# The root of the norms in four VectorE operations instead of six, and the last block's rows multiplied by the final weights before their root is known

## The chip, the cores and the metric

The kernel runs on one core of one Trainium2 chip. The metric is the device time of one execution in microseconds (us), and kernels are compared by the medians of several. A core has a matrix engine (TensorE, here PE, whose weight loads are shown as PEld), three engines for element-wise work (VectorE or DVE, ScalarE or ACT, GpSimd or POOL), and an engine that issues most of the transfers (SyncE or SP). Each engine runs its own list of instructions in a fixed order and waits at an instruction until its inputs and its output buffer are free.

## The reference

One layer of a decoder with 1,024 tokens of width 1,024 and 16 learned meta tokens ahead of them:

```python
def rmsnorm(x, g):
    x32 = x.astype(jnp.float32)
    y = x32 * lax.rsqrt(jnp.mean(x32 * x32, axis=-1, keepdims=True) + EPS)
    return (y * g.astype(jnp.float32)).astype(x.dtype)
...
        h = h + hybrid_mixer(rmsnorm(h, attn_norm_g[l]), pos, topk, w_in[l], mla_q_norm_g[l], w_uq[l],
                             mla_kv_norm_g[l], w_ukv[l], w_o[l])
        h = h + swiglu(rmsnorm(h, ffn_norm_g[l]), w_gate[l], w_up[l], w_down[l])
    h = rmsnorm(h, final_norm_g)
    return h[:, N_META:t]
```

`hybrid_mixer` has two groups of heads on one input projection: eight heads of latent attention (MLA, dense and causal, with a norm of its own on each latent), and eight heads of sparse attention (DSA), in which an indexer scores all keys and each query keeps the 256 best. The outputs of both go through one output projection `w_o`. `swiglu` is the feed-forward part (FFN) with a hidden width of 2,816. What matters for this change is `rmsnorm`: per row, the mean of the squares plus EPS, its inverse root, and the product with the weights `g`.

## The kernel before

The 1,024 rows are eight blocks of 128, one row for each partition. Blocks 0 to 2 are called A here (`BLK_A`), blocks 3 to 7 B (`BLK_B`). The stages follow each other like this in the profile: the norm of the input, the projections and the index scores, with the first searches for the 256 best keys (0 to about 330 us); attention of A, and its output projection (to about 500); attention of B with the FFN of A interleaved (to about 966, the last product of the FFN of A is added at 977.94); the output projection of B (to about 1070); the FFN of B by seven products of block sums (to about 1490); the last norms (to the end). All products are made of three fp32r matmuls (`three`, L195 to L198), for which each operand is split into a rounded part and a rest (`split`, L186 to L193): ACT writes the rounded part (`wH`, `woh`, `us` and so on), and POOL or DVE subtracts it (`wL`, `wol`).

**The root.** `rstd` (L151 to L162) takes the sum of squares `ss` and gives 1/sqrt(ss/n + EPS). DVE makes the mean (L155), ACT its square root (L156), DVE the reciprocal r (L157), and then one step of Newton's iteration in four operations, r(1.5 - 0.5 v r r) (L158 to L161). These tiles have one column a block (128x1), so the operations are short. It is called 40 times: in `norm_in` (L278) for the nine norms of the input (tile `rs`), in `latent` (L517) for 17 latents (tile `rsc`), in `out_proj` (L1060) once for the three blocks of A together (width 3) and once for each block of B, and in `last_norm` (L1285) for the eight blocks. Its users: `norm_in` and `latent` scale rows; `out_proj` writes `un` (L1065, 128x512, twice a block), which PE transposes (L1068) as the input of the FFN; `last_norm` scales the rows that go out (L1290 to L1294).

**The last norm.** For each half of a block ACT sums squares (`yj`, L1279). When both halves are there, DVE adds the sums (L1284) and `rstd` follows. The first 512 columns are scaled and weighted by DVE in one operation (L1293), the second 512 by ACT (L1290) and POOL (L1291), except in the last block, where DVE does both halves. For A this happens at about 970 to 1000 us, for B at the end.

**The search.** The 256 best keys of a query are found bit by bit: a pass counts the keys above a bound, and the bound moves. For blocks 6 and 7 ACT makes the passes (L382, tile `js`, with two small operations L383 and L385 between), and DVE ends the search (L445 to L458), after which the bias of that block's DSA scores is known: PE makes scores (L790), DVE adds the bias and takes the extreme (L792), ACT makes the exponentials (L799), DVE and POOL split them into fp16 parts (`hl`, L819 and L821), a transfer transposes them (`pT`), and PE multiplies by the values (L830 to L832).

**The output projection of B.** `w_o` comes in 32 pieces of 128x256 through two buffers `wor`, each through one chain: transfer, ACT (`woh`, L188), POOL (`wol`, L191), matmuls.

**What sets the order.** The code names no order across stages beyond its loops and generators. The program is built with the framework's own timeline scheduling, which estimates when each operation could run and writes every engine's list by that. So a change of the number or form of operations anywhere can put other instructions into another order on every engine, even on those that the change doesn't name.

## Time and profile before

| | us |
|---|---|
| median of 3 runs | 1516.27 |
| lowest and highest of them | 1514.63, 1522.13 |
| profiled execution, its time | 1515.98 |
| profiled execution, span from first to last instruction | 1514.2 |
| mean granted clock of TensorE, share of full speed | 0.972 |

The rows of the profile are times of one execution, counted from its first instruction. "Busy" is the sum of durations on an engine; matmuls overlap, so that the busy time of a matmul in a row is longer than its distance to the next one. The view of waits shows how long an engine stood at an instruction and which other instruction ended that. The chain of work that ended last is followed back from the end of the program.

### The profile page before, as it was taken

What the parts mean: (1) busy time and instruction counts of PE and PEld (TensorE: products, weight loads), DVE (VectorE), ACT (ScalarE), POOL (GpSimd) and SP (SyncE); (2) the same over time, 40 slices, a digit from 0 to 9 for tenths busy, and PEclk for the clock granted to TensorE, in tenths of its full rate; (3) what the DMA queues carried; (4) which work ended last, traced back from release to release, by engine and by line L of the source; (5) the groups of instructions that cost most, each with busy time, mean ns of one, the idle gap of its engine ahead of it and who ended that gap; (6) DMA issues with size and microseconds to landing.
All of it is one profiled execution on the core that took longest, in us unless ns stands there. A gap on an engine that the chain in (4) does not pass through costs nothing. (4 is left out here: it accounts for less than half of the span.)

```text
span 1514.2 us, 29979 instructions
## 1 busy us (share of the span) xinstructions
PE 1405.1 (93%) x10320; PEld 1295.3 (86%) x10320; DVE 1105.3 (73%) x2714; ACT 922.9 (61%) x2264; POOL 892.8 (59%) x1185
## 2 busy tenths in 40 slices
PE   6999998899989899899999999888799999999996
PEld 5999998897778789798888888788789999999995
DVE  6878989948886875957766666736676777777766
ACT  5666578897889889788544444434544444444444
POOL 2564555212404588687878778643846666666653
PEclk9999999999999799999999999998899999999999
DMA  6113265224434688687879998741222222222211
GB/s 177 55 48 85 73 143 134 52 89 131 130 102 123 146 193 166 147 171 175 182 157 222 200 203 181 188 140 50 65 62 84 84 84 84 79 76 83 84 56 70
DMA packets 353737, 180.74 MB, mean 119 GB/s; under 512 B 196560, under 2 KB 341344, under 8 KB 353584
## 3 DMA queue, kind: packets, MB, share of 16 engines
q1 hardware_dynamic: 353584, 178.82, 47.7%
q8 instruction: 81, 1.33, 0.4%
q14 instruction: 72, 0.59, 0.1%
HBM read 120.77 MB, written 21.30 MB: 94 GB/s over the span
## 5 line engine op out<-in xcount | busy, mean ns | idle before, releaser
L191 POOL TENSOR_TENSOR wL<-raw,wH 128x256 fp32r<-128x256 f32 x352 | 286.1, 846 | 59.0 <-ACT wH L188 55.3
L821 POOL TENSOR_TENSOR hl<-pd,hl 128x260 f16<-128x260 f32 (+5 forms) x256 | 168.8, 689 | 71.1 <-ACT hl L817 31.8
L191 POOL TENSOR_TENSOR wsl<-raw,wsh 128x256 fp32r<-128x256 f32 x132 | 120.3, 940 | 94.1 <-ACT wsh L188 53.6
L196 PE MATMUL b<-wh,uH 128*128 128x256 f32 (+3 forms) x568 | 169.2, 298 | 6.3 <-DVE mlo L318 3.2
L198 PE MATMUL b<-wh,uL 128*128 128x256 f32 (+3 forms) x568 | 168.5, 297 | 0.0
L197 PE MATMUL b<-wl,uH 128*128 128x256 f32 (+3 forms) x568 | 168.1, 296 | 0.1
L188 ACT ACTIVATE wH<-raw 128x1024 fp32r<-128x1024 f32 x88 | 91.8, 1054 | 79.4 <-PE b L198 20.0
L196 PE MATMUL b<-us,wsh 128*128 128x320 f32 x440 | 136.1, 313 | 1.5 <-DVE oh L1251 1.1
L197 PE MATMUL b<-us,wsh 128*128 128x320 f32 x440 | 136.4, 311 | 0.0
L198 PE MATMUL b<-us,wsl 128*128 128x320 f32 x440 | 134.2, 310 | 0.0
L196 PE MATMUL b<-ua,wH 128*128 128x384 f32 x352 | 122.1, 347 | 3.4 <-ACT wH L188 3.4
L382 ACT ACTIVATE js<-sc,bs 128x528 bf16<-128x528 int16 (+7 forms) x128 | 120.9, 945 | 4.7 <-DVE sc L437 2.4
L197 PE MATMUL b<-ua,wH 128*128 128x384 f32 x352 | 121.2, 344 | 0.0
L198 PE MATMUL b<-ua,wL 128*128 128x384 f32 x352 | 120.7, 344 | 0.1
L196 PE MATMUL b<-wH,hH 128*128 128x512 f32 x282 | 113.5, 403 | 3.9 <-DVE oh L1171 2.1
L196 PEld LDWEIGHTS b<-wh,uH 128*128 128x128 f32 x568 | 108.7, 191 | 8.3 <-DVE mlo L318 3.9
L197 PE MATMUL b<-wL,hH 128*128 128x512 f32 x282 | 112.1, 397 | 0.0
L198 PE MATMUL b<-wH,hL 128*128 128x512 f32 x282 | 110.1, 398 | 0.4 <-DVE hL L193 0.4
L197 PEld LDWEIGHTS b<-wl,uH 128*128 128x128 f32 x568 | 108.8, 191 | 0.5 <-DVE wl L193 0.3
L198 PEld LDWEIGHTS b<-wh,uL 128*128 128x128 f32 x568 | 108.6, 191 | 0.4 <-DVE uL L193 0.2
L1240 DVE TENSOR_TENSOR oh<-b,oh 128x512 f32<-128x512 f32 x110 | 74.5, 685 | 46.3 <-PE b L198 45.4
L799 ACT ACTIVATE pd<-pd,sm 128x528 f32<-128x528 f32 (+4 forms) x80 | 75.7, 946 | 48.6 <-DVE sm L797 46.1
(410 smaller groups left out, 4848.0 us busy)
## 6 DMA issues: line engine op xcount, KB each, us to landing
raw<-in_w_gate SPq DMA_DIRECT2D x44, 512.0 KB, 4.0
raw<-in_w_up SPq DMA_DIRECT2D x44, 512.0 KB, 4.1
raw<-in_w_down SPq DMA_DIRECT2D x44, 512.0 KB, 3.7
wor<-in_w_o SPq DMA_DIRECT2D x64, 128.0 KB, 2.5
wraw<-in_w_in SPq DMA_DIRECT2D x40, 128.0 KB, 2.4
vh<-v_x SPq DMA_DIRECT2D x16, 288.0 KB, 3.8
xt<-in_x SPq DMA_DIRECT2D x8, 512.0 KB, 4.4
ks_x<-st SPq DMA_DIRECT2D x32, 128.0 KB, 2.1
```

The source lines that it names most:

```text
L188: S.activation(h, src, AF.Copy)
L191: G.tensor_sub(l[:, c], src[:, c], h[:, c])
L196: PE.matmul(o, lh, rh, start=first, stop=False, **kw)
L197: PE.matmul(o, lh, rl, start=False, stop=False, **kw)
L198: PE.matmul(o, ll, rh, start=False, stop=last, **kw)
L382: S.activation(act_junk()[:, :n_keys(b)], y[b], AF.Sign, bias=cols[0], accum_out=cnt)
L799: S.activation(pb, pb, AF.Exp, bias=mn, scale=-1.0, accum_out=z)
L821: G.tensor_sub(pl_[:, c], pb[:, c], ph[:, c])
L1240: V.tensor_add(oh[t][:, cs], po, oh[t][:, cs])
```

## The change

In `rstd` the mean is made with the factor -4 (and -4 EPS), ACT's square root takes it with scale -1, and the reciprocal is then half of 1/sqrt. The Newton step becomes two fused operations (`scalar_tensor_tensor`, two steps of arithmetic on one pass): r r v in one, and (that + 3) r in the other. With width 3 the first of them stays two products. So DVE runs four operations instead of six in 39 of the 40 calls, and five in the one of width 3: 79 fewer.

In `last_norm`, for the last block (7) alone, the rows are multiplied by `gl` into a buffer `raw` of the FFN's weights before the root is made: DVE columns 0 to 511 and 768 to 1023, POOL columns 512 to 767. When the root is there, DVE scales columns 0 to 511 and ACT columns 512 to 1023. The list of DVE has 78 instructions fewer in all (2,528 after 2,606), ACT and POOL have one more each.

```diff
-        V.tensor_scalar(v[:, 0], ss, 1.0 / n, EPS, op0=OP.mult, op1=OP.add)
-        S.activation(v[:, 1], v[:, 0], AF.Sqrt)
+        V.tensor_scalar(v[:, 0], ss, -4.0 / n, -4.0 * EPS, op0=OP.mult, op1=OP.add)
+        S.activation(v[:, 1], v[:, 0], AF.Sqrt, scale=-1.0)
         V.reciprocal(v[:, 1], v[:, 1])
-        V.tensor_mul(v[:, 2], v[:, 1], v[:, 1])
-        V.tensor_mul(v[:, 2], v[:, 2], v[:, 0])
-        V.tensor_scalar(v[:, 2], v[:, 2], -0.5, 1.5, op0=OP.mult, op1=OP.add)
-        V.tensor_mul(v[:, 3], v[:, 1], v[:, 2])
+        if w == 1:
+            V.scalar_tensor_tensor(v[:, 2], v[:, 1], v[:, 1], v[:, 0], op0=OP.mult, op1=OP.mult)
+        else:
+            V.tensor_mul(v[:, 2], v[:, 1], v[:, 1])
+            V.tensor_mul(v[:, 2], v[:, 2], v[:, 0])
+        V.scalar_tensor_tensor(v[:, 3], v[:, 2], 3.0, v[:, 1], op0=OP.add, op1=OP.mult)
         return v[:, 3]
...
+            if t == NB - 1:
+
+                yg = fu.tile([P, D], F32, name="raw", bufs=RAW_N)
+                V.tensor_mul(yg[:, 0:512], oh[t][:, 0:512], gl[:, 0:512])
+                G.tensor_mul(yg[:, 512:768], oh[t][:, 512:768], gl[:, 512:768])
+                V.tensor_mul(yg[:, 768:], oh[t][:, 768:], gl[:, 768:])
...
             for k in range(2):
+                if t == NB - 1:
+                    y = yg[:, k * 512:(k + 1) * 512]
+                    if k:
+                        S.activation(y, y, AF.Copy, scale=r)
+                    else:
+                        V.tensor_scalar(y, y, r, None, op0=OP.mult)
+                    ld(out[0, t * P:(t + 1) * P, k * 512:(k + 1) * 512], y)
+                    continue
                 y = oh[t][:, k * 512:(k + 1) * 512]
                 g = gl[:, k * 512:(k + 1) * 512]
-                if k and t < NB - 1:
+                if k:
```

Lines of the changed kernel are 3 later than those of before from `rstd`'s end on, and 6 to 17 later in `last_norm`. The scheduling writes other orders, mostly between about 200 and 1070 us; in the FFN of B (1100 to 1490) the lists agree. Three places:

DVE at the end of the program, before: the last block's root `rs_20008` and both halves of its rows.

```order
L1284 TENSOR_TENSOR ss_20006<-ss_19993 128x1
L161 TENSOR_TENSOR rs_19972<-rs_19972 128x1
L155 TENSOR_SCALAR rs_20008<-ss_20006 128x1
L1293 SCALAR_TENSOR_TENSOR oh_5127<-oh_5127,rs_19972,gl 128x512
L157 RECIPROCAL rs_20008<-rs_20008 128x1
L158 TENSOR_TENSOR rs_20008<-rs_20008 128x1
L159 TENSOR_TENSOR rs_20008<-rs_20008 128x1
L160 TENSOR_SCALAR rs_20008<-rs_20008 128x1
L161 TENSOR_TENSOR rs_20008<-rs_20008 128x1
L1293 SCALAR_TENSOR_TENSOR oh_5128<-oh_5128,rs_20008,gl 128x512 x2
```

DVE there with the change (`oh_5076` is the last block, `rs_19935` its root, `rs_19897` that of block 6):

```order
L1243 TENSOR_TENSOR oh_5076<-b_19919,oh_5076 128x512
L1310 SCALAR_TENSOR_TENSOR oh_5074<-oh_5074,rs_19863,gl 128x512
L158 RECIPROCAL rs_19897<-rs_19897 128x1
L1291 TENSOR_TENSOR raw<-oh_5076,gl 128x256
L1293 TENSOR_TENSOR ss_19933<-ss_19916 128x1
L160 SCALAR_TENSOR_TENSOR rs_19897<-rs_19897 128x1
L156 TENSOR_SCALAR rs_19935<-ss_19933 128x1
L164 SCALAR_TENSOR_TENSOR rs_19897<-rs_19897 128x1
L1310 SCALAR_TENSOR_TENSOR oh_5075<-oh_5075,rs_19897,gl 128x512
L158 RECIPROCAL rs_19935<-rs_19935 128x1
L160 SCALAR_TENSOR_TENSOR rs_19935<-rs_19935 128x1
L164 SCALAR_TENSOR_TENSOR rs_19935<-rs_19935 128x1
```

One operation of 128x512 follows this (L1301, the scaling of the last block's first half); the products with the weights stand ahead of the root, and block 6's root now stands behind the product of 256 columns.

ACT at the last passes of the search for block 7, before (the last pass is the one of `js` in the sixth row):

```order
L382 ACTIVATE js,bs_8237<-sc_69,bs_8237 128x1040
L383 ACTIVATE bs_8237<-bs_8237,th_8238 128x1
L1156 ACTIVATE sg<-b_13510 128x384
L188 ACTIVATE wH<-raw 128x1024
L385 ACTIVATE bs_8237<-bs_8237 128x1
L382 ACTIVATE js,bs_8237<-sc_69,bs_8237 128x1040
L833 ACTIVATE oh_5124<-b_10469 128x64
L799 ACTIVATE pd,zs<-pd,sm 128x912
```

ACT there with the change, where `js` is L385 and the split of FFN weights L191:

```order
L385 ACTIVATE js,bs_8184<-sc_69,bs_8184 128x1040
L191 ACTIVATE hH<-sg 128x384
L386 ACTIVATE bs_8184<-bs_8184,th_8185 128x1
L388 ACTIVATE bs_8184<-bs_8184 128x1
L191 ACTIVATE wH<-raw 128x1024
L385 ACTIVATE js,bs_8184<-sc_69,bs_8184 128x1040
L836 ACTIVATE oh_5075<-b_10558 128x64
L191 ACTIVATE kH_7454<-b_10639 128x400
```

In the whole list of ACT, 36 splits `wH` stand ahead of that last pass since the start of the FFN of A with the change, 33 before; exponentials (L799 before) ahead of it are 92 with the change, 91 before. PE's list moves with it: ahead of its 410th matmul of scores (L790 before) 50 more matmuls of the FFN's first factors (`ua`) and 27 more of its second (`wH,hH`) stand there with the change, ahead of the last one (the 560th) 48 and 6 more; ahead of the 400th it was 14 fewer and none. And 30 matmuls of the second factors that followed attention's last matmul of values before stand ahead of it now.

POOL where attention's last splits end and the pieces of `w_o` begin, before (`oh_5121` to `oh_5123` are the blocks of A):

```order
L821 TENSOR_TENSOR hl_7511<-pd,hl_7511 128x260 x4
L191 TENSOR_TENSOR wL<-raw,wH 128x256 x4
L191 TENSOR_TENSOR wol_14839<-wor,woh_14838 128x256
L191 TENSOR_TENSOR wol_14841<-wor,woh_14840 128x256
L191 TENSOR_TENSOR wol_14843<-wor,woh_14842 128x256
L191 TENSOR_TENSOR wol_14845<-wor,woh_14844 128x256
L1291 TENSOR_TENSOR oh_5121<-oh_5121,gl 128x512
L191 TENSOR_TENSOR wsl_14824<-raw,wsh_14823 128x256 x2
L191 TENSOR_TENSOR wsl_14826<-raw,wsh_14825 128x256 x2
L191 TENSOR_TENSOR wol_14847<-wor,woh_14846 128x256
L191 TENSOR_TENSOR wsl_14828<-sc_68,wsh_14827 128x256 x2
L191 TENSOR_TENSOR wol_14849<-wor,woh_14848 128x256
```

POOL there with the change (`oh_5069` to `oh_5071` are the blocks of A):

```order
L824 TENSOR_TENSOR hl_7459<-pd,hl_7459 128x260 x4
L194 TENSOR_TENSOR wol_14786<-wor,woh_14785 128x256
L194 TENSOR_TENSOR wol_14788<-wor,woh_14787 128x256
L1308 TENSOR_TENSOR oh_5069<-oh_5069,gl 128x512
L194 TENSOR_TENSOR wol_14790<-wor,woh_14789 128x256
L194 TENSOR_TENSOR wol_14792<-wor,woh_14791 128x256
L194 TENSOR_TENSOR wsl_14771<-raw,wsh_14770 128x256 x2
L194 TENSOR_TENSOR wsl_14773<-raw,wsh_14772 128x256 x2
L1308 TENSOR_TENSOR oh_5070<-oh_5070,gl 128x512
L194 TENSOR_TENSOR wsl_14775<-sc_68,wsh_14774 128x256 x2
L1308 TENSOR_TENSOR oh_5071<-oh_5071,gl 128x512
L194 TENSOR_TENSOR wol_14794<-wor,woh_14793 128x256
```

The first product of the last norm of A stands behind two pieces of `w_o` instead of four, all three of them behind four instead of seven.

## Rows read from the trace of the kernel before

**Rows 1.** The page's first part: busy time of each engine, share of the span and instructions.

```profile
PE 1405.1 (93%) x10320; PEld 1295.3 (86%) x10320; DVE 1105.3 (73%) x2714; ACT 922.9 (61%) x2264; POOL 892.8 (59%) x1185
```

**Rows 2.** Busy time by stretch: from and to (us), length, busy time of each engine with its instructions, granted clock of TensorE as a share of full speed, share of the DMA engines, GB/s.

```profile
600.00:740.00 140.00, 129.25 (x1073) 116.59 (x1072) 106.07 (x254) 116.62 (x255) 109.53 (x150) 0.99 0.79 170
740.00:966.00 226.00, 212.66 (x1815) 191.86 (x1814) 152.44 (x365) 100.99 (x206) 184.79 (x258) 0.99 0.85 184
966.00:1070.00 104.00, 84.94 (x602) 78.93 (x599) 60.26 (x148) 48.10 (x143) 45.44 (x56) 0.86 0.38 112
1070.00:1490.00 420.00, 416.08 (x2454) 385.03 (x2454) 293.85 (x424) 179.01 (x350) 263.68 (x302) 1.00 0.26 76
1500.00:1514.20 14.20, 3.97 (x15) 2.31 (x14) 10.59 (x34) 5.23 (x14) 3.97 (x4) 0.83 0.44 167
```

**Rows 3.** The chain that ended last from 960 to 1030 us, pieces in order of time: start, us, what.

```profile
960.71 4.59 DMA pT<-hl
...
977.94 0.69 DVE oh L1171
...
1002.76 2.37 DMA wor<-in_w_o
1005.22 0.43 ACT ckH L188
1005.71 0.75 POOL ckL L191
1006.48 2.38 DMA wor<-in_w_o
...
1010.20 3.13 DMA wor<-in_w_o
```

**Rows 4.** The waits of PE from 1030 to 1070 us: who waited for whom, us in all, times, the longest.

```profile
PE b L1068 <- DVE un L1065: 12.0, 2, 7.8
```

**Rows 5.** All engines in order of time at the end of the program: start, duration, engine, line, operation, tiles; in brackets the idle time before it and what ended it.

```profile
1506.97 0.72 ACT L1290 ACTIVATE oh<-oh,rs 128x512 f32<-128x512 f32 x1 [0.52 <-DVE rs L161]
...
1507.77 1.26 POOL L1291 TENSOR_TENSOR oh<-oh,gl 128x512 f32<-128x512 f32 x1 [1.42 <-ACT oh L1290]
1507.82 0.16 DVE L157 RECIPROCAL rs<-rs 128x1 f32<-128x1 f32 x1
1508.01 1.03 DVE L158 TENSOR_TENSOR rs<-rs 128x1 f32<-128x1 f32 x1
1509.08 0.16 DVE L159 TENSOR_TENSOR rs<-rs 128x1 f32<-128x1 f32 x1
...
1509.66 1.42 DVE L1293 SCALAR_TENSOR_TENSOR oh<-oh,rs,gl 128x512 f32<-128x512 f32 x2
```

**Rows 6.** The instructions of the tile `rs` and, in the last row, a fused operation of the same size on the search's tile `bs`: line, engine, operation, count, shortest, median and longest duration in ns, first and last start in us.

```profile
L158 DVE TENSOR_TENSOR rs<-rs x23: 145/159/1064, 6.1 to 1508.0; 128x1 f32<-128x1 f32 x21, 16x1 f32<-16x1 f32 x1, 128x3 f32<-128x3 f32 x1
L159 DVE TENSOR_TENSOR rs<-rs x23: 142/159/1254, 6.3 to 1509.1; 128x1 f32<-128x1 f32 x21, 16x1 f32<-16x1 f32 x1, 128x3 f32<-128x3 f32 x1
L160 DVE TENSOR_SCALAR rs<-rs x23: 136/154/169, 6.5 to 1509.3; 128x1 f32<-128x1 f32 x21, 16x1 f32<-16x1 f32 x1, 128x3 f32<-128x3 f32 x1
L161 DVE TENSOR_TENSOR rs<-rs x23: 146/159/693, 6.7 to 1509.5; 128x1 f32<-128x1 f32 x21, 16x1 f32<-16x1 f32 x1, 128x3 f32<-128x3 f32 x1
...
L406 DVE SCALAR_TENSOR_TENSOR bs<-bs x64: 140/160/846, 191.7 to 629.7; 128x2 f32<-128x2 f32 x32, 128x1 f32<-128x1 f32 x32
```

**Rows 7.** DVE in order of time where the first of the norms of the input ends, columns as in rows 5.

```profile
6.69 0.15 DVE L161 TENSOR_TENSOR rs<-rs 16x1 f32<-16x1 f32 x1
7.00 1.27 DVE L283 SCALAR_TENSOR_TENSOR xt<-xt,rs,gb 16x1024 f32<-16x1024 f32 x1 [0.16 <-DMA gb<-in_attn_norm_g]
```

**Rows 8.** DVE in order of time where the last `un` is made (1060 to 1068 us), columns as in rows 5.

```profile
1062.66 0.15 DVE L157 RECIPROCAL rs<-rs 128x1 f32<-128x1 f32 x1
1062.84 0.42 DVE L1103 TENSOR_TENSOR ts<-b,ts 128x256 f32<-128x256 f32 x1
...
1063.38 0.65 DVE L159 TENSOR_TENSOR rs<-rs 128x1 f32<-128x1 f32 x1
...
1065.63 1.99 DVE L1065 SCALAR_TENSOR_TENSOR un<-oh,rs,gbf 128x512 f32<-128x512 f32 x2
```

**Rows 9.** ACT in order of time at the last passes of the search for block 7.

```profile
738.76 1.06 ACT L188 ACTIVATE wH<-raw 128x1024 fp32r<-128x1024 f32 x1 [2.09 <-DMA raw<-in_w_gate]
...
740.03 1.16 ACT L382 ACTIVATE js<-sc,bs 128x1040 bf16<-128x1040 uint16 x1
```

**Rows 10.** DVE after it: the end of the search and the first scores that use it.

```profile
759.39 0.64 DVE L458 TENSOR_TENSOR sc<-sc,cbias 128x128 bf16<-128x128 bf16 x1
759.95 0.50 DVE L792 CUSTOM_DVE_ANT_0 pd<-b,sc 128x348 f32<-128x348 f32 x1
```

**Rows 11.** PE in order of time from 759 us on: matmuls of the FFN of A's first factors, one matmul of scores, and two of the second factors.

```profile
759.35 0.34 PE L196 MATMUL b<-ua,wH 128*128 128x384 f32 x1
759.52 0.34 PE L197 MATMUL b<-ua,wH 128*128 128x384 f32 x1
...
760.52 0.43 PE L790 MATMUL b<-kH,qH 128*128 128x344 f32 x1 [0.48 <-DVE sm L792]
...
761.71 0.39 PE L196 MATMUL b<-wH,hH 128*128 128x512 f32 x1
761.94 0.40 PE L197 MATMUL b<-wL,hH 128*128 128x512 f32 x1
```

**Rows 12.** The waits of PE from 600 to 966 us.

```profile
PE b L790 <- DVE sm L792: 10.3, 10, 2.7
PE b L830 <- DMA pT<-hl: 4.6, 3, 2.4
```

**Rows 13.** ACT in order of time: the splits of the first two pieces of `w_o` for B, and that of the last piece.

```profile
967.32 0.72 ACT L188 ACTIVATE woh<-wor 128x256 fp32r<-128x256 f32 x2 [0.76 <-DVE oh L845]
...
1026.57 0.42 ACT L188 ACTIVATE wsh<-wor 128x256 fp32r<-128x256 f32 x1 [0.84 <-POOL wsl L191]
```

## The prediction

> **What bounds the kernel now.** I read the page's first part first: PE is busy for 1405 of 1514 us, DVE for 1105, ACT for 923 and POOL for 893 [rows 1]. So an operation that leaves DVE is worth nothing as such. It is worth something where PE, or the end of the program, waits for DVE, and only there. Next comes the table by stretches, since the share of 93% is a mean over stages that differ [rows 2]. In the FFN of B PE is busy for 416.1 of 420 us; in that stretch the instructions have the same order before and after and hold no root, so I give it no change. The stretches that can move are three. From 600 to 966 us (attention of B with the FFN of A filled in) PE is busy for 341.9 of 366 us, so it has some 24 us of idle time spread over the stretch. From 966 to 1070 (the output projection of B) it idles for 19 us. In the last 14.2 us PE works for 4 us and DVE for 10.6: the end belongs to DVE.
>
> What ends the waits there? Between 966 and 1030 the chain of waits goes round one loop: a transfer of a piece of `w_o` of 2.4 to 3.1 us, ACT's split 0.43, POOL's rest 0.75, and the next transfer [rows 3]. Between 1030 and 1070 PE waits for 12.0 us in two waits for `un`, which DVE makes behind a root [rows 4]. At the end it is the last block's root and its two halves [rows 5]. These are the three places where the change can pay directly. Everything else that it does, it does by way of the order.
>
> **The direct part: what the roots lose.** The four operations of the Newton step have medians of 159, 159, 154 and 159 ns [rows 6]. The trace has no fused operation on the root's tile, but one of the same size on the search's tile, median 160 ns [rows 6]. So fusing costs nothing per operation and each root gets shorter by two of them, 0.31 us; 79 fewer operations are about 12.4 us of DVE time in all. Of this nearly all lies beside PE's work. What lies on a path:
>
> The first norm of the input: `xt` (L283) is ready to start behind the root at about 6.85, but starts at 7.00 because the row of weights `gb` lands only then [rows 7]. The shorter root gains nothing for that block; for the next ones some tenths at most. I take -0.5 us, from -1 to 0. The cover is that transfer: were it earlier, 0.3 us a block would show.
>
> The last `un` of B: its root runs from 1062.66, L159 alone takes 0.65 there, and the two `un` of 1.99 us start at 1065.63 with PE waiting [rows 4, 8]. In the new order the root of this block has its two fused operations in a row right behind a sum of 256 columns, and `un` directly behind these: two short operations (0.3), the held one (0.5) and three sums of 0.42, which now stand behind `un`, drop out of the way, of which some had room anyway. I take -1.5 us, from -3 to 0: at nought the inputs of the block come no sooner and the three sums only fill idle time.
>
> The end. Before: reciprocal at 1507.82, L158 at 1508.01 for 1.03 us, L159 at 1509.08, L160 and L161, and both halves on DVE from 1509.66 for 1.42 us, done at 1511.08 [rows 5]. After: reciprocal, two fused operations, one scaling of 512 columns on DVE with the other half on ACT beside it (0.72 for a scaling on ACT [rows 5]). Gone from the path are at most one half (0.71), two short operations (0.38 with their gaps) and the excess of L158 over its median (0.87). Against that, 768 columns of products with the weights now stand on DVE ahead of the sum L1284, of which the 512 can run while ACT sums squares, and the 256 (some 0.4 us) stand ahead of it. The three are 2.0 us; where two roots of the blocks ahead lose such an excess of 0.87 too, 3.7. But L158 took 1.03 us instead of 0.16, and it started while POOL's L1291 ran from 1507.77 for 1.26 us, and ended when that ended [rows 5]. L158 and L159 have maxima of 1064 and 1254 ns, and L160, which has one tensor input, has 169 [rows 6]. POOL now has one more product in this stretch, and DVE more operations on two tensors (the three products, the fused first step is one too). If two of those are held for a whole product of POOL (1.26 less 0.16, 1.1 each) and the 256 columns stand in the way (0.4), that is +2.6, less the half that is gone (0.71) +1.9. I take -1, from -4 to +2.
>
> This is where a rule speaks against the change. The Trainium skill, page "SBUF — State Buffer", section "Who interferes with whom", says that a VectorE instruction with two inputs in SBUF contends with a GpSimd instruction that reads SBUF, since its second input comes through a port pair that the two share, and that whoever issues first keeps it for the whole instruction while the other blocks. The trace agrees with it in L158: 1.03 us under POOL's product against a median of 0.159. By this rule alone the end would come out at +1.9 us, without it at -3.7; it shifts the third place only.
>
> **The indirect part: what the order does.** The lists of all engines differ between about 200 and 1070 us. DVE having less to do does not decide there; where the rare resource is put does. I look for the point that others wait for. It is the search for block 7. Its last pass on ACT starts at 740.03, DVE ends it at 759.39 to 760.03, and the first score operation of block 7 is at 759.95 [rows 9, 10]. PE reaches its first scores of that block just there, waiting 0.48 us for the bank [rows 11]: ACT and PE arrive nearly together. With the change three more splits of 1.06 us [rows 9] and one more exponential (about 1 us) stand ahead of that last pass on ACT, so the search ends some 4 us later if ACT has no idle time ahead of it; it has some (2.09 us in front of one of these splits [rows 9]), so from 0 to +4.
>
> On PE the matmuls of the FFN of A cost 0.17 us each for the first factors and 0.23 for the second, by the distance between starts [rows 11]. Ahead of the 410th matmul of scores, where block 7's scores begin, 50 and 27 more of them stand with the change: 8.5 + 6.2 = 14.7 us. Ahead of the 400th it was 2.4 us less than before. Ahead of the last one it is 48 and 6: 8.2 + 1.4 = 9.5 us. So the scheduling expects the search to end later against PE, and fills the time with FFN; attention's own work for block 7 is pushed behind it. PE idles for 13.3 us between 740 and 966 [rows 2]; in the longer stretch from 600 on its waits for score banks are 10.3 us and those for transposed exponentials 4.6 [rows 12]. A denser fill ahead leaves these later waits where they are; work that is moved ahead is missing later as a filler. So the end of attention moves by something between 0 (idle time swallows it) and +9.5, with the search's own +4 in the middle. I take +4 for it.
>
> **The stretch behind attention.** What was moved ahead is missing afterwards: 30 matmuls of second factors that came after attention's last values now come before them, 6.9 us of PE. Before, they ran beside the first pieces of `w_o`: the last transfer of attention lands at 965.30, the FFN's last sum is at 977.94 [rows 3], and the first two pieces are split at 967.32, the last one at 1026.57 [rows 13]. From 1002 on the loop alone sets the pace, about 3.7 us for two pieces through two buffers [rows 3], so those matmuls were under cover of a chain that doesn't get shorter. What can change is the chain's first part. POOL's three products of the last norm of A (1.26 us for such a one [rows 5]) stand now behind the second, fourth and fourth piece instead of the fourth, seventh and seventh. That puts up to two of them, 2.5 us, earlier in front of pieces; on the other hand the norms behind the FFN's last sums are ready sooner against attention's end. I take +1, from -2 to +3.
>
> **The sum.** Against the profiled execution of 1515.98: +4 (end of attention), +1 (pieces of `w_o`), -1.5 (`un`), -1 (end), -0.5 (start) are +2, so 1518.0. The median of the three runs is 1516.27, 0.3 us above that execution, which I don't add. A measurement of this kernel can tell about 0.5%, 7.6 us, from no change: faster means below 1508.7, slower above 1523.9.
>
> **Rivals.** First, the order is neutral and only the direct gains stay: -1.5, -2 and -0.5 and nothing else, about 1512, within the bound. For it: idle time of 24 us in the stretch of attention. Against it: ACT and PE both get more ahead of the one point that attention waits for.
>
> Second, slower: the FFN work that is put ahead of block 7's scores costs its full 9.5 us, because PE works 94% of the stretch and the later waits for banks and transfers stay as they are, and the pieces of `w_o` start late and lose their +3. With -3 for the direct part that is +9.5, about 1525.5. It decides from the point where attention's last transfer lands about 10 us later than now, after 975 us. For it: the counts above. Against it: work done ahead need not be done later, and 6.9 us of it was hidden.
>
> Third, faster: the 30 matmuls and the late norms of A were not under cover. Between the first two splits at 967.32 and the steady loop, ACT also sums squares and the FFN's last sums come at 977.94 [rows 3, 13]; if this is what slows the chain's start, an FFN that ends before attention lets the chain start at its own pace, some 8 us sooner, with attention's end where it was: -8 and -3 give about 1505. Against it: the two buffers, not ACT, set the pace from 1002 on.
>
> Fourth, the change doesn't do what it says: a fused operation is held by POOL as long as the two that it replaces, and DVE's extra products stand in front of the sums. Then the end gives nothing or +1.9, and the sum is some 1521, within the bound.
>
> **The numbers.** Chances: the forecast with the fourth case, which falls into the same band, 0.42; the first rival 0.22; slower 0.22; faster 0.14. Faster by over 0.5% is 0.14, within 0.64, slower 0.22. The range reaches from the third case's edge to past the second: its low end is 1508.5, where the first rival with all its direct bounds ends (-4, -3, -1 give 1508.0), its high end 1527, the second rival with the held end.
>
> **What would show it.** In the profile after: the last `js` pass (740.03 now) at 740 to 745 and the first block-7 score operation (759.95 now) at 760 to 765; attention's last transfer landing (965.3 now) at 965 to 975; the pieces of `w_o` again some 59 us from the first split to the last (967.32 to 1026.57 now); the wait of PE for `un` below 12.0 us in all; the FFN of B at 416 us of busy time in 420; and from the last addition to the last DVE operation less than now. The fused operations should have medians of 0.16 us, with single ones held up to 1.3 us under POOL's products. I am wrong if the stretch before 600 us moves by more than 2 us, if attention's end comes earlier, or if the chain of `w_o` gets shorter by more than 3 us.

## The result, and the profile after

| | before | with the change |
|---|---|---|
| median, us (4 runs each) | 1517.22 | 1536.51 |
| lowest and highest, us | 1514.63, 1522.13 | 1534.05, 1538.82 |
| profiled execution: its time, span, us | 1515.98, 1514.2 | 1535.28, 1533.5 |

The ratio is 1.0133, with a 95% interval from 1.0115 to 1.0151. The changed kernel is slower by 1.3%, and its time lies outside the range that was forecast. Two executions of the experiments, one of 6508 us in e4 and one of 2697 us in e10, are slow ones and stay out of every figure below.

The first question is where the 19.3 us between the two spans appear. The first and last starts of a few lines answer it. With the change (line, engine, operation, count; shortest, median and longest duration in ns; first and last start in us), for the sums of the output projections, `un`, and the sums of the FFN of B:

```profile
L1055 DVE TENSOR_TENSOR oh<-b,xr x32: 405/424/425, 449.6 to 1076.4; 128x256 f32<-128x256 f32 x32
L1068 DVE SCALAR_TENSOR_TENSOR un<-oh,rs,gbf x16: 737/752/1223, 495.3 to 1084.5; 128x512 f32<-128x512 f32 x16
L1243 DVE TENSOR_TENSOR oh<-b,oh x110: 667/685/693, 1129.2 to 1522.6; 128x512 f32<-128x512 f32 x110
```

The same lines before start first and last at 448.0 and 1054.1, 494.2 and 1066.4, 1112.2 and 1504.9. At 449 and 495 us the change is 1.6 and 1.1 us behind, at the end of the output projection of B 22.3, at the last `un` 18.1, at the last sum of the FFN 17.6, at the end 19.3. So the time is lost between 500 and 1076 us, and what follows gives some of it back and then loses a little. In between lies the point that the prediction had named, block 7's search. ACT's last pass of it and DVE's end of it, with the change:

```profile
759.28 1.15 ACT L385 ACTIVATE js<-sc,bs 128x1040 bf16<-128x1040 uint16 x1
...
778.06 0.22 DVE L461 TENSOR_TENSOR sc<-sc,cbias 128x128 bf16<-128x128 bf16 x1
778.19 0.51 DVE L795 CUSTOM_DVE_ANT_0 pd<-b,sc 128x348 f32<-128x348 f32 x1
```

They answer to 740.03, 759.39 and 759.95 in [rows 9, 10]: 19.3 us later, and block 7's first score operation 18.2 later. In front of it DVE is at work on the search until 778.28, so the search releases DVE's first operation on these scores. But PE has no idle time to show for it. From block 6's first pass to block 7's first score operation, before and with the change (columns as in [rows 2]):

```profile
444.83:759.95 315.12, 291.35 (x2399) 264.18 (x2397) 234.05 (x598) 263.05 (x599) 226.15 (x317) 0.96 0.73 163
446.40:778.19 331.79, 305.47 (x2468) 277.15 (x2467) 243.15 (x603) 266.46 (x604) 231.43 (x326) 0.96 0.70 161
```

PE works for 14.1 us more there, on 69 matmuls more, and idles for 26.3 us instead of 23.8. So PE's own list reaches this point as late as the search does: its next score matmul of the block starts at 779.82 with no idle time in front, where it had waited 0.48 us before [rows 11]. The whole difference, from mark to mark:

| from, to | before, us | with the change, us | difference |
|---|---|---|---|
| start, first ACT pass of block 6 | 444.8 | 446.4 | +1.6 |
| ... block 7's first score operation | 315.1 | 331.8 | +16.7 |
| ... attention's last matmul of values | 206.2 | 207.3 | +1.1 |
| ... last sum of the output projection of B | 88.0 | 90.9 | +2.9 |
| ... last `un` | 12.3 | 8.1 | -4.2 |
| ... last sum of the FFN of B | 438.5 | 438.1 | -0.4 |
| ... end | 9.2 | 10.9 | +1.7 |

The 16.7 us can be read pass by pass. ACT makes 16 passes for the first half of a search (upper bits) and 16 for the second. Between the halves POOL turns ACT's result into a bound with two operations on 128x1 (`bs`, L389 and L390 before, L392 and L393 now), and DVE prepares the second half (L436 and L437, now L439 and L440). I call this the handoff. (The same two POOL operations stand behind the second half too, ahead of DVE's end of the search; and ACT searches for blocks 3 and 4 in this way as well, earlier.) Block 6's before, ACT, POOL and DVE in order of time:

```profile
508.64 1.05 ACT L382 ACTIVATE js<-sc,bs 128x912 bf16<-128x912 int16 x1
...
511.54 0.29 ACT L383 ACTIVATE bs<-bs,th 128x1 f32<-128x1 f32 x1
511.92 0.22 POOL L389 TENSOR_SCALAR bs<-bs 128x1 f32<-128x1 f32 x1 [1.36 <-ACT bs L383]
512.23 0.19 POOL L390 TENSOR_TENSOR bs<-bs 128x1 f32<-128x1 f32 x1
512.50 1.15 DVE L436 TENSOR_SCALAR_CACHE_REDUCE jk<-sc,bs 128x912 bf16<-128x912 int16 x1
...
513.58 1.32 DVE L437 SCALAR_TENSOR_TENSOR sc<-sc,bs 128x912 uint16<-128x912 int16 x1
517.18 1.04 ACT L382 ACTIVATE js<-sc,bs 128x912 bf16<-128x912 uint16 x1
```

8.5 us from pass to pass, and POOL takes 0.6 of them. With the change ACT's pass starts at 514.33 and its small operation at 518.30; POOL from then on:

```profile
518.47 2.80 POOL L194 TENSOR_TENSOR wL<-raw,wH 128x256 fp32r<-128x256 f32 x4 [0.21 <-ACT wH L191]
521.23 0.22 POOL L392 TENSOR_SCALAR bs<-bs 128x1 f32<-128x1 f32 x1
521.41 2.80 POOL L194 TENSOR_TENSOR wL<-raw,wH 128x256 fp32r<-128x256 f32 x4
524.18 1.78 POOL L824 TENSOR_TENSOR hl<-pd,hl 128x228 f16<-128x228 f32 x3
525.92 0.19 POOL L393 TENSOR_TENSOR bs<-bs 128x1 f32<-128x1 f32 x1
526.07 3.20 POOL L824 TENSOR_TENSOR hl<-pd,hl 128x228 f16<-128x228 f32 x5
529.22 5.58 POOL L194 TENSOR_TENSOR wL<-raw,wH 128x256 fp32r<-128x256 f32 x8
```

and DVE, then ACT's next pass:

```profile
527.48 1.15 DVE L439 TENSOR_SCALAR_CACHE_REDUCE jk<-sc,bs 128x912 bf16<-128x912 int16 x1
...
528.55 7.21 DVE L440 SCALAR_TENSOR_TENSOR sc<-sc,bs 128x912 uint16<-128x912 int16 x1
...
535.80 1.05 ACT L385 ACTIVATE js<-sc,bs 128x912 bf16<-128x912 uint16 x1 [5.33 <-DVE sc L440]
```

The reader sees one small operation of POOL behind four splits of FFN weights and the other behind four more and three parts of exponentials: POOL takes 7.5 us where it took 0.6. Then DVE's L440, on two tensors, lasts 7.21 us instead of 1.32, and ends 0.96 us after POOL's row of thirteen operations without a gap (526.07 to 534.80). From pass to pass it is 21.5 us. For block 7 it is the same picture:

```profile
681.62 1.15 ACT L385 ACTIVATE js<-sc,bs 128x1040 bf16<-128x1040 int16 x1
...
688.60 0.54 POOL L392 TENSOR_SCALAR bs<-bs 128x1 f32<-128x1 f32 x1
689.11 5.60 POOL L194 TENSOR_TENSOR wL<-raw,wH 128x256 fp32r<-128x256 f32 x8
694.67 0.19 POOL L393 TENSOR_TENSOR bs<-bs 128x1 f32<-128x1 f32 x1
```

Eight splits stand between the two, which before stood next to each other (661.84 and 662.14); DVE's L439 then starts at 699.82, since DVE had been held in a small operation (L845, 4.87 us from 691.99) and was late with all that followed. From 681.62 to the next pass at 702.40 it is 20.8 us, and 6.5 before. The two handoffs grew by 12.9 and 14.3 us, 27.2 together. The passes around them changed too: block 6's halves by +4.1 and -3.1 us, the gap to block 7 by +0.2, block 7's halves by +7.3 and -17.9, the end of the search by -1.0. These and 27.2 are the 16.7, but for rounding. So the search lost 27.2 us in the handoffs and another 11.6 in passes, and got 22.0 back, most of it in block 7's last 16 passes (74.8 us before, 56.9 now).

ACT's busy time, summed over the same pieces, says where these come from:

| ACT, us | before | with the change |
|---|---|---|
| block 6's first pass to block 7's last | 295.2 | 312.9 |
| busy in it (instructions) | 254.7 (582) | 261.0 (593) |
| idle in it | 40.5 | 51.9 |
| the two handoffs: busy, idle | 11.9, 3.2 | 22.2, 20.0 |
| block 7's last half: busy (instructions), idle | 63.4 (140), 11.4 | 50.6 (111), 6.3 |

Of the 17.7 us, 6.3 are more work ahead of the last pass and 11.4 more idle time. The longer handoffs hold 10.4 us more of ACT's other work, and block 7's last half is short because 29 instructions fewer stand in it (12.8 us) and ACT idles less there (5.1). What is left of the handoffs' 27.2 us as idle time is 16.8, of which the other pieces give 5.4 back.

The chain of work that ended last goes through both handoffs, but not through the end of block 7's search. With the change it holds these pieces, among others (start, us, what):

```profile
528.83 6.86 issue
...
692.13 4.64 issue
...
774.27 3.80 DMA raw<-in_w_gate
```

The first two lie where L440 and L845 are held. From 734 to 787 the chain runs through PE's matmuls and the FFN's weights (POOL `wL`, transfers into `raw`), past the end of the search at 778. In the kernel before the chain can be followed back to 960 only, so there is nothing to compare it with.

In the stretches that answer to [rows 2], moved by the delay, PE idles for 26.2 us in the output projection of B (19.1 before), and the FFN of B is as it was (417.3 of 420 us against 416.1):

```profile
985.50:1087.50 102.00, 75.79 (x523) 69.80 (x519) 52.65 (x120) 45.49 (x139) 44.90 (x55) 0.87 0.38 114
1087.50:1507.50 420.00, 417.33 (x2459) 386.26 (x2458) 292.37 (x425) 179.16 (x351) 263.48 (x303) 1.00 0.26 76
```

The root's operations and PE's wait for `un` (to [rows 6] and [rows 4]):

```profile
L160 DVE SCALAR_TENSOR_TENSOR rs<-rs x22: 205/220/1215, 6.2 to 1527.1; 128x1 f32<-128x1 f32 x21, 16x1 f32<-16x1 f32 x1
L164 DVE SCALAR_TENSOR_TENSOR rs<-rs x23: 144/159/682, 6.5 to 1528.4; 128x1 f32<-128x1 f32 x21, 16x1 f32<-16x1 f32 x1, 128x3 f32<-128x3 f32 x1
```

```profile
PE b L1071 <- DVE un L1068: 10.4, 2, 8.2
```

The first fused operation, on three columns, has a median of 220 ns, the second 159. So a root of 128x1 is shorter by 631 - 379 = 252 ns of DVE's time, by the medians. And the end of the program (to [rows 5]):

```profile
1524.69 1.21 DVE L1293 TENSOR_TENSOR ss<-ss 128x1 f32<-128x1 f32 x1
...
1526.93 0.15 DVE L158 RECIPROCAL rs<-rs 128x1 f32<-128x1 f32 x1
1527.06 1.26 POOL L1308 TENSOR_TENSOR oh<-oh,gl 128x512 f32<-128x512 f32 x1 [1.17 <-ACT oh L1307]
1527.12 1.22 DVE L160 SCALAR_TENSOR_TENSOR rs<-rs 128x1 f32<-128x1 f32 x1
1528.37 0.16 DVE L164 SCALAR_TENSOR_TENSOR rs<-rs 128x1 f32<-128x1 f32 x1
1528.56 0.49 DVE L1301 TENSOR_SCALAR raw<-raw,rs 128x512 f32<-128x512 f32 x1
```

The last block's scaling is short now (0.49 beside ACT's half instead of 1.42), but its root's first fused operation is held under POOL's product as L158 was (1.22 against 1.03). What is new on the path is the product of 256 columns (0.87) and behind it the sum L1293, held for 1.21 us where L1284 took 0.15: from the FFN's last sum to the mean of the last root it is 3.4 us instead of 1.9, and to the end 10.9 instead of 9.2.

### The profile page after: what moved, and what is told of

The parts are those of the page before. It is cut to its first block, busy times and chain, and to the rows that moved or that the text cites. A ratio compares the mean times of both kernels' runs of the same rounds, so it can differ in the third digit from the quotient of the medians.

```text
span 1533.5 us, 29891 instructions
## 1 busy us (share of the span) xinstructions
PE 1409.0 (92%) x10320; PEld 1294.8 (84%) x10320; DVE 1101.8 (72%) x2636; ACT 926.1 (60%) x2265; POOL 884.0 (58%) x1186
## 4 chain that ended last, share of the span: by engine, by line
PE 46%; DVE 18%; DMA 12%; POOL 8%; ACT 8%; issue 6%; SPq 1%; POOLq 0%; ACTq 0%; DVEq 0%
PE b L199 13%; PE b L201 13%; PE b L200 13%; DMA pT<-hl 6%; POOL wL L194 3%; DVE jk L400 3%; POOL hl L824 3%; PE b L793 2%; DMA wor<-in_w_o 2%; ACT js L385 1%; DMA wraw<-in_w_in 1%; DVE pd L795 1%; DVE bs L409 1%; DMA raw<-in_w_gate 1%; PE b L357 1%
## 5 line engine op out<-in xcount | busy, mean ns | idle before, releaser
L194 POOL TENSOR_TENSOR wL<-raw,wH 128x256 fp32r<-128x256 f32 x352 | 282.6, 836 | 65.0 <-ACT wH L191 62.5
L191 ACT ACTIVATE wH<-raw 128x1024 fp32r<-128x1024 f32 x88 | 91.5, 1053 | 73.6 <-PE b L201 18.8
L385 ACT ACTIVATE js<-sc,bs 128x528 bf16<-128x528 int16 (+7 forms) x128 | 120.8, 944 | 14.6 <-DVE sc L440 10.4
L199 PEld LDWEIGHTS b<-wh,uH 128*128 128x128 f32 x568 | 109.0, 192 | 10.8 <-DVE vw L171 5.5
```

The source lines that it names most:

```text
L191: S.activation(h, src, AF.Copy)
L194: G.tensor_sub(l[:, c], src[:, c], h[:, c])
L199: PE.matmul(o, lh, rh, start=first, stop=False, **kw)
L385: S.activation(act_junk()[:, :n_keys(b)], y[b], AF.Sign, bias=cols[0], accum_out=cnt)
```

## Experiments

Theory H, for handoff: the shorter root changes the estimates by which the lists are written, the two operations of POOL between the halves of a search land between other work, DVE is held behind it, the search of block 7 ends later, and attention ends as much later. Rivals: L (the last block's part costs it), O (the fused operations are slower on the chip), F (the FFN's matmuls that stand ahead of block 7's scores cost it). All numbers first, then run by run. Handoffs, first score operation of block 7, the stretch from there to attention's last values, and the time from the FFN's last sum to the end are from the traces; the time beside them is that of the traced execution, the ratio that of all runs to the kernel before on the same chip, with its 95% interval. Times of different chips are compared by these ratios. The change, e1 and e5 have four executions, e11 two, the others 8 to 12.

| run | handoffs, blocks 6 and 7 | first score | stretch | end | traced, us | ratio |
|---|---|---|---|---|---|---|
| before | 8.5, 6.5 | 760.0 | 206.2 | 9.2 | 1516.0 | 1 |
| the change | 21.5, 20.8 | 778.2 | 207.3 | 10.9 | 1535.3 | 1.0133 (1.0115 to 1.0151) |
| e1 root only | 21.2, 20.7 | 771.9 | 211.0 | 8.5 | 1527.9 | 1.0126 (1.0088 to 1.0163) |
| e2 last block only | 8.9, 6.5 | 760.7 | 205.3 | 10.8 | 1514.6 | 0.9996 (0.9979 to 1.0014) |
| e3 change, handoff on DVE | 7.4, 13.8 | 766.0 | 204.1 | 10.9 | 1514.7 | 0.9989 (0.9971 to 1.0007) |
| e4 change, early roots as before | 11.8, 22.9 | 769.5 | 205.6 | 10.9 | 1520.6 | 1.0048 (1.0029 to 1.0067) |
| e5 before, handoff lengthened | 15.3, 27.8 | 778.5 | 202.3 | 9.2 | 1528.5 | 1.0076 (1.0058 to 1.0095) |
| e6 before, handoff on DVE | 6.7, 5.8 | 769.9 | 206.5 | 9.2 | 1521.6 | 1.0054 (1.0037 to 1.0071) |
| e7 root only, handoff on DVE | 7.6, 13.7 | 768.6 | 207.4 | 8.8 | 1519.7 | 0.9978 (0.9962 to 0.9993) |
| e8 root only, handoff on ACT | 11.8, 9.4 | 763.4 | 203.9 | 8.8 | 1514.0 | 0.9983 (0.9967 to 0.9999) |
| e9 shorter root late only | 8.9, 6.5 | 758.4 | 206.8 | 8.4 | 1508.9 | 0.9971 (0.9957 to 0.9985) |
| e10 e9 and last block | 8.7, 6.5 | 759.4 | 208.4 | 11.1 | 1514.7 | 0.9997 (0.9980 to 1.0015) |
| e11 change, less FFN | 21.2, 13.2 | 789.2 | 193.0 | 10.9 | 1529.0 | 1.0122 (1.0091 to 1.0153) |
| e12 before, less FFN | 8.7, 6.2 | 773.6 | 198.5 | 9.2 | 1522.6 | 1.0030 (1.0013 to 1.0047) |

**e1, the root alone.** The diff of `rstd` as in the change, `last_norm` as before.

> The shorter root everywhere, the last block's rows as before. Theory H (handoff): the time was lost in the search of blocks 6 and 7, whose two small operations on POOL between the halves now stand between splits of FFN weights; the lists of POOL are the same here as with the whole change, so attention ends some 19 us later than before and the time is 1532 to 1537 us. Rival L (last block): the products with the weights ahead of the root cost it; then this one is at 1514 to 1519 us.

The median is 1531.23 us against 1514.13, just below the range that H gave, a ratio as with the whole change. The handoffs are as long. The lists are those of the change up to the last norms, and still the first score comes 6.3 us sooner than there and attention's end 2.6: so far do two executions of the same lists differ at these marks. So the root's part alone brings the loss, and L has fallen. That each root takes less of DVE's time is in the rows above.

**e2, the last block alone.** `rstd` as before, `last_norm` as in the change.

> The last block's part alone, with the root in six operations; up to the end all lists stand as before. Theory H: 1515 to 1520 us, attention ends within 1 us of before, and what is left of a difference is made in the last 15 us. Rival L: 1530 us or more.

1514.05 us against 1514.13, 1 us below the range that H gave and far from L; attention ends where it did. In the traced execution the end takes 10.8 us instead of 9.2, which is lost in the spread of the times (1509.9 to 1519.2).

**e3, the handoff on DVE.** The changed kernel with

```diff
-                G.tensor_scalar(up, up, 0.5, None, op0=OP.mult)
-                G.tensor_sub(cols[1], up, cols[0])
+                V.tensor_scalar(up, up, 0.5, None, op0=OP.mult)
+                V.tensor_sub(cols[1], up, cols[0])
```

These lines serve both halves of all four searches on ACT, so eight pairs of operations move: the handoffs, and the pairs behind the second halves.

> The whole change, with the two operations between the halves of ACT's search on DVE instead of POOL, where they stand next to each other. Theory H: from the last pass of the first half to the first of the second 6 to 11 us for blocks 6 and 7 (21.5 and 20.8 with the change), and 1514 to 1523 us. Rival F (the FFN's matmuls that stand ahead of block 7's scores cost it) and rival O (fused operations are slower on the chip than the ones they replace): 1530 us or more, since neither is touched.

1512.70 us against 1514.13: the loss is gone (1.3 us below the range that H gave), with all fused operations and the last block's part in place. That is against O and for H. The first score is still 6.1 us later than before; the last `un` alone gives 4.8 us back. Block 6's handoff is 7.4 us; block 7's is 13.8, more than expected, since DVE's second operation of the handoff was held (DVE, then POOL, in order of time):

```profile
666.25 8.33 DVE L393 TENSOR_TENSOR bs<-bs 128x1 f32<-128x1 f32 x1
```

```profile
662.56 4.92 POOL L194 TENSOR_TENSOR wL<-raw,wH 128x256 fp32r<-128x256 f32 x7
667.43 0.75 POOL L194 TENSOR_TENSOR ckL<-wor,ckH 128x256 fp32r<-128x256 f32 x1
668.13 3.03 POOL L824 TENSOR_TENSOR hl<-pd,hl 128x264 f16<-128x264 f32 x5
671.11 0.73 POOL L194 TENSOR_TENSOR ckL<-wor,ckH 128x256 fp32r<-128x256 f32 x1
671.79 2.77 POOL L194 TENSOR_TENSOR wL<-raw,wH 128x256 fp32r<-128x256 f32 x4
```

An operation on one column waits until POOL's row of operations ends, at 674.56. But this run doesn't tell H from F: with the handoff off POOL, the FFN's matmuls stand ahead of the 410th score matmul about as before (11 fewer of the first factors), so F's cause is gone with H's.

**e4, the early roots as before.** A second `rstd` with six operations, used by `norm_in` and `latent`.

> The whole change, but the norms of the input and of the latents with the root in six operations. The lists are as before up to about 445 us. POOL's two operations of the search have one split of weights between them for block 6 (4 x 256 columns, with the change these and three exponentials' parts), one small split and three exponentials' parts for block 7. Theory H: handoffs of 10 to 17 us, and a time between the two kernels, 1518 to 1531 us. Rival O: about 1517 us or less, since 52 of the 79 operations are back and only 27 are fewer.

1521.22 against 1514.13, in the range that H gave, with 27 operations fewer than before. Block 7's handoff, 22.9 us, is longer than expected. A loss in proportion to the number of fused roots would look the same here, so against O it is the other runs that speak.

**e5, the handoff lengthened in the kernel before.** Nothing of the change is in it:

```diff
+                for _ in range(4 if b > 5 and first == 0.0 else 0):
+                    G.tensor_scalar(up, up, 1.0, None, op0=OP.mult)
                 G.tensor_scalar(up, up, 0.5, None, op0=OP.mult)
                 G.tensor_sub(cols[1], up, cols[0])
```

> The kernel before, with nothing of the change. In the search of blocks 6 and 7 four more operations of 128x1 (a product with 1.0) stand on POOL ahead of the two between the halves. They take about 0.2 us each, but in POOL's list the rest of the handoff now comes behind three exponentials' parts and four splits (block 6) and behind several of each (block 7). Theory H: handoffs of 13 to 22 us instead of 8.5 and 6.5, attention's end 6 to 18 us later, and a time of 1520 to 1532 us. Rival O (operations of the root) and rival L (last block): 1512 to 1517 us, since both are as before. Rival F (FFN matmuls ahead of the scores): the stretch from block 7's first score to attention's last values gets longer than 206 us; under H it stays within 2 us of that.

1527.81 against 1515.47. Without any fused operation, an edit to two handoffs alone makes the kernel before slower by 0.8%, where the shorter root made it slower by 1.3% (e1). Block 7's first score comes 18.5 us later than before, as with the change. Its handoff of 27.8 us is longer than expected: DVE's operation was held again,

```profile
688.26 6.51 DVE L439 SCALAR_TENSOR_TENSOR sc<-sc,bs 128x1040 uint16<-128x1040 int16 x1
```

against 1.6 for this operation in the kernel before. The stretch behind it is 202.3 us, 4 shorter than before, a little more than H allowed; F, as I had put it, wanted it longer. That was no fair test: matmuls that stand ahead of the score lengthen what lies in front of it. There PE is busy for 303.0 of 334.5 us, 11.7 more than before and idle for 7.7 more, so here at least the 7.7 are not PE's own work.

**e6, the kernel before with the handoff on DVE.** The diff of e3 on the kernel before.

> The kernel before with the two operations between the halves on DVE. Theory H: the handoffs were short already (8.5 and 6.5 us), so there is nothing to win: 6 to 14 us each, and 1508 to 1518 us. If moving these two operations off POOL is worth something by itself, apart from the handoffs, it is 1500 us or less.

1524.54 against 1515.47: H was wrong here. The handoffs are short, 6.7 and 5.8 us, and the search ends 10 us late all the same: it starts 4.2 us later (449.0 against 444.8), block 7's last 16 passes take 78.7 us instead of 74.8, and from the last of them to the first score it is 23.7 instead of 19.9. A change of engine for two small operations writes other lists everywhere, and these cost 0.5%. Handoffs are one way to delay the search, not the only one.

**e7 and e8, the root alone with the handoff on DVE and on ACT.** The second has

```diff
-                G.tensor_scalar(up, up, 0.5, None, op0=OP.mult)
-                G.tensor_sub(cols[1], up, cols[0])
+                S.activation(up, up, AF.Copy, scale=0.5)
+                S.activation(cols[1], cols[0], AF.Identity, scale=-1.0, bias=up)
```

> The shorter root everywhere, the last block's rows as before, the two operations on DVE. As in the run of the whole change with them on DVE, but without the last block's part, which cost 1.5 us at the end in the traces so far (10.8 and 10.9 us from the last sum's start to the end with it, 9.3 before, 8.5 with the shorter root alone). Theory H: 1508 to 1515 us, that is 0 to 4 us below before, handoffs of 7 to 14 us. Rival O: 1530 us.

> The shorter root everywhere, the last block's rows as before, the two operations between the halves on ACT, which has made the count just before, so no other engine stands between. Theory H: handoffs of 5 to 15 us (what is left is DVE's two operations of 1040 columns and what stands ahead of them), 1506 to 1516 us. Rival O: 1530 us.

1511.64 and 1511.93 against 1515.47, both as H has it and far from O, though the first score is still 8.7 and 3.5 us later than before. (The traced execution of e7 is the slowest of its eleven.)

**e9 and e10, the shorter root where it can't reorder the search.** Six operations everywhere but in the output projection and the last norms of B; e10 with the last block's part.

```diff
-                r = rstd(wo, tot, D, P, "rs2")
+                r = (rstd if blocks[0] else rstd6)(wo, tot, D, P, "rs2")
...
-            r = rstd(fu, tot, D, P, "rs3")
+            r = (rstd if t >= NA else rstd6)(fu, tot, D, P, "rs3")
```

> The shorter root only where it is late: in the output projection of B and in the last norms of B; all other roots in six operations, the last block's rows as before. Every list stands as before up to about 1040 us, so the search can't move. Theory H with the direct gains as the traces show them (from the last sum of the output projection to the last un 7.5 to 8.1 us with the shorter root, 11.1 to 12.3 without; from the FFN's last sum to the end 8.5 to 8.9 against 9.2 to 9.3): 4 to 5.5 us less than before, a ratio of 0.9965, with search and attention within 2 us of before. Rival O (the shorter root is no faster on the chip): a ratio of 1.000 or more.

> The same with the last block's part of the change. From the FFN's last sum to the end 10.8 us as in the other runs with that part, so 1.5 to 2.3 us more than without it: a ratio of 0.998 to before. If the last block's products pay, it is below 0.996.

e9 takes 1508.96 us against 1512.89, a ratio of 0.9971 where 0.9965 was expected, and is faster than both kernels. The search is where it was (its last pass at 738.5, 740.0 before), PE waits for `un` for less,

```profile
PE b L1084 <- DVE un L1081: 7.7, 3, 7.0
```

against 12.0 in [rows 4], and the end is 8.4 us. With the last block's part all that is gone, 0.9997: some 4 us by the ratios, of which the end shows 2.7, 11.1 against 8.4.

**e11 and e12, less work for PE.** To tell F from H, the FFN of A leaves out one of its three products by the second factors, in the changed kernel and in the one before (so the output lacks that part):

```diff
-                        three(po, hid[g][0][:, sl], hid[g][1][:, sl], wdn[g][0][:, cs], wdn[g][1][:, cs],
-                              g == fs[0], g == fs[-1])
+                        PE.matmul(po, hid[g][0][:, sl], wdn[g][0][:, cs], start=g == fs[0], stop=False)
+                        PE.matmul(po, hid[g][1][:, sl], wdn[g][0][:, cs], start=False, stop=g == fs[-1])
```

> The whole change, but the FFN of A leaves out the product of the hidden part's rest with the second factors (132 of 396 matmuls of 512 columns, 30 us of PE at 0.23 us). Rival F (FFN on PE is what lengthens the attention of B): the stretch from block 7's first score to attention's last values falls from 207 us to 195 or less, and attention ends at 975 us or sooner. Theory H: that stretch stays between 202 and 209 us, and attention's end follows from the end of the search, whose handoff for block 6 is cut up as with the change (18 to 22 us).

> The kernel before with the same product of the FFN of A left out (30 us of PE). In POOL's list the two operations between the halves stand together for both blocks. If the handoffs make the difference between the two kernels, they are 7 to 11 us here, block 7's first score comes at 757 to 768 us, the stretch to attention's last values is 190 to 197 us as in the changed kernel without that product (193.0), attention ends at 948 to 964, and the time is 1498 to 1514 us: the distance to the changed kernel without the product (1530.7) stays at 17 us or more. Rival F (PE's FFN work makes the difference): with 30 us of it gone from both, the distance falls below 10 us, so 1521 us or more here.

Neither theory is met. In e11 the stretch is 193.0 us, as F had it and against H; but attention's last values come at 982.1, not at 975 or sooner, since the search ends later still, and the time is 1530.71. In e12 the handoffs are short and the search is nevertheless 13.6 us later than before (up to the last pass ACT is busy for 7.1 us more, with five more splits `wH` ahead of it); the time is 1520.62. The distance of the pair is 10 us by the medians, 14 by the ratios, since the two ran on different chips: between what the two theories wanted. What they do show: with 30 us of PE's work gone the kernel before is no faster (1.0030), and block 7's stretch is shorter by 8 to 14 us. So PE's load counts in that stretch, and its gain is lost again in when the stretch begins.

## Why the prediction was wrong

The step that failed is in the part on the order: "With the change three more splits of 1.06 us [rows 9] and one more exponential (about 1 us) stand ahead of that last pass on ACT, so the search ends some 4 us later if ACT has no idle time ahead of it; it has some (2.09 us in front of one of these splits [rows 9]), so from 0 to +4". The count was right: the three splits and the exponential are 4.2 of the 6.3 us that ACT works more. What failed is the idle time. It was to swallow work, and it grew by 11.4 us. The step took the search for a chain on ACT alone. Twice in each search the chain leaves ACT and goes through POOL and DVE, and there the lists had changed far more: seven and eight pieces of other work stand between the two small operations of POOL, where none stood before, and each small operation has more ahead of it. In the two handoffs ACT idles for 20.0 us instead of 3.2. The bound "from 0 to +4" for the search, and with it "+4, from 0 to +9.5" for attention's end, had no row for that. Measured: 19.3 us at the last pass, 18.2 at the first score, 19.4 at attention's end (e1, with the same lists: 14.1, 11.9 and 16.7).

The same step failed on PE. The prediction had counted 14.7 us of matmuls ahead of block 7's first scores, and PE does work for 14.1 us more there. It let idle time swallow part of that as well, but PE's idle time didn't fall (23.8 us before, 26.3 with the change). Its own sign of being wrong came early: block 6's last half begins at 535.80 instead of 517.18, so the stretch before 600 us had moved by far more than 2 us.

The place was right as a mark. In the ten kernels with the FFN whole, e1 to e10, the stretch behind block 7's first score is 202.3 to 211.0 us whatever the first score's time, 758 to 779, so what moves this mark moves attention's end. What is shown is that the loss comes with the root's part alone (e1) and with its early calls (e9, which keeps the late ones, loses nothing), that it goes when the pairs of the search leave POOL (e3, e7, e8), and that a loss of 0.8% can be made in the kernel before by an edit to the handoff alone (e5). Each of these edits also writes other lists. e6 and e12 lose 5 to 9 us with short handoffs.

Not shown is which of two things in the new lists sets the time: the late search, or PE's fuller list ahead of the scores. The second rival, which is the latter, had the sign, and its point of decision was met: attention's last transfer lands at 982.8, after 975. The stretch behind the first score, 207.3 us against 206.2, says nothing against it, since those matmuls stand ahead of that score. They are missing afterwards, where PE idles longer in the output projection of B. For the handoff speaks e5 with its 7.7 us of idle time on PE. But in e3, e7 and e8, where the loss is gone, PE's list ahead of the first score is as before too (2384, 2384 and 2400 matmuls, 2399 before, 2468 with the change). That the scheduling puts FFN work there because it expects the handoff late would join the two; no run shows it.

The other steps, by their terms. The start, -0.5: +1.6 in the traced executions. Kernels whose lists are the same there as before (e2, e9, e10) have 445.8, 443.7 and 444.9 us against 444.8, so executions differ by 2 us on this mark and the term can't be told from nothing. The last `un`, -1.5 from -3 to 0: -4.2, and 7.4 to 8.1 us from the last sum to the last `un` in the nine kernels with the shorter root there, 11.1 to 12.3 in the five without. The root's own part had the forecast size: from its reciprocal to the first `un` 1.4 us instead of 3.0, although an operation in it is held as before (L164, 0.60 us). The rest lies ahead of the root, where the two `un` of the block before now stand ahead of the last sum. The end, -1 from -4 to +2: +1.7. The fourth rival was right about it. The Trainium skill's page "SBUF — State Buffer", section "Who interferes with whom", lets an operation of VectorE on two tensors in SBUF wait for one of GpSimd that reads SBUF, and the fused first step did so for 1.22 us under a product of 1.26. The two parts come apart: the shorter root makes the end 0.4 to 0.8 us shorter (8.4 to 8.8), the products ahead of the root make it 1.6 to 2.7 us longer (e2 and e10, against before and e9). The pieces of `w_o`, +1 from -2 to +3: +2.9, at the bound, but +0.3 in e1 with the same lists there, so this term can't be told from nothing either. The price of the first fused operation, 160 ns from a row with two tensors: 220 ns with three.

## What to carry to other kernels

Where a scheduler writes the lists, a change of a few short operations is first of all a new order, and its direct gain (here some 4 us, e9) is smaller than what a new order costs (0.5 to 1.3% here). Before such a change is costed, follow the chain that releases the most work through every engine that it visits, down to operations of 0.2 us, and look in the new lists at what now stands in front of each; the engine on which most of the chain lies is not the one to look at alone. Work that a list puts ahead of such a point is counted in full unless a row shows idle time that it fills. An edit that must not disturb is best put where only later lists can change, as in e9.

## What was not expected of the hardware

A DVE operation on two tensors in SBUF can be held not for one operation of POOL but for a whole row of them without a gap: 7.21 us (L440, 1.32 before), ending 0.96 us after the last of thirteen operations of POOL without a gap; 8.33 us for one on 128x1 (0.15 at its shortest); 6.51 us in e5. Each of the fourteen traces has one or two such operations of over 4.5 us between 500 and 720 us, the kernel before too (a rest of 128x384, L193, 5.22 us at 683.14), and which operation it hits depends on the order. All twenty of them end 1.1 us or less after the end of such a row. Others pass between two of POOL's operations after less than 1 us (L406 in the kernel before: 0.77 us at 519.45, under eight splits); what decides it, no run here shows. One with a single tensor and a scalar per row was held too (L845, 128x4, 4.87 us).
